# One layer of a flow-matching backbone on one core: x transposed by token tile between the adaLN slabs, constant products on TensorE, and the second adaLN slabs in other buffers

## The chip, the core and the metric

The kernel runs on one core of one Trainium2 chip. The metric is the device time of one execution, in microseconds (us). Before the change it was measured three times: 1683.73, 1684.34 and 1685.08, median 1684.34. The profile shows one more execution of 1684.17 us; its span, from the first to the last instruction, is 1682.5 us. Engines are named as in the profile: PE (TensorE), DVE (VectorE), ACT (ScalarE), POOL (GpSimd) and SP, whose queue issues most DMAs.

## The reference

One layer is applied to 128 context tokens and 256 latent tokens of width 2048. Only the start matters here: the adaLN modulation, the first norm and the input projection.

```python
def _adaln(cond, ada_w, ada_b):
    mod = jax.nn.silu(cond) @ ada_w + ada_b
    return mod.reshape(cond.shape[0], N_MOD, D_MODEL)
...
    shift_a, scale_a, gate_a, shift_f, scale_f, gate_f = [mod[:, i][:, None, :] for i in range(N_MOD)]
    h = _rmsnorm(x, norm_w[0]) * (1 + scale_a) + shift_a
    proj = h @ w_in
    q, k, v, o, g, u = jnp.split(proj, [M, 2 * M, 3 * M, 4 * M, 4 * M + N_GATES * N_HEADS], axis=-1)
...
    mix = jnp.concatenate([hm, hp], axis=-1) @ w_out
    x = x + gate_a * _rmsnorm(mix, norm_w[1])
    h = _rmsnorm(x, norm_w[2]) * (1 + scale_f) + shift_f
    y = jnp.square(jax.nn.relu(h @ w1)) @ w2
    x = x + gate_f * _rmsnorm(y, norm_w[3])
```

The condition is `c_ctx` for the context tokens and `c` for the latent ones; `ada_w` is 2048 x 12288. All inputs are float32.

## The kernel before

All 384 tokens are worked on together: three token tiles of 128, and 16 feature tiles of 128. Every large product is made of three products of split numbers (high x high, high x low, low x high); a weight tile or h is split by ACT, which writes the high half, and DVE, which subtracts to get the low half (L135 and L136 for weights, L448 and L449 for h).

The opening. SP issues the loads of the two conditions (L80, L81), of the constants (L82: identity, ones and a selector) and of x (L88, 1 MB for each token tile). POOL issues the loads of the parameters. Then come the adaLN slabs, 512 KB each: four slabs hold the 16 x 128 rows of one pair of feature tiles of `ada_w` for one of scale and shift. Function `ada_mat` multiplies a slab with cT, the conditions after silu, in four small products that lie side by side on PE (L257; the profile counts two rows for each float32 product, so x8 is one slab). Function `ada_rows` then copies the sums out of PSUM on ACT (L269), and two small products (L273) add the four groups and turn them; `ada_finish` adds the bias on DVE (L281, L286). The result is `mod`. The generator `first_ada` strings these pieces together and stops after each slab; `next(ada0)` runs it to its next stop. The string `X_ORDER` says when: "a" is one such piece, "t" transposes one feature tile of x for the three token tiles (three PE transposes, L403, into one PSUM bank, and a copy of 384 columns by DVE or ACT, L411 and L409), and "b" spreads the inverse norms `rx` over a row, a diagonal matrix on DVE (L207, `dg_rx`) and a product with ones on PE (L209, `bc_rx`), copied to `rbc` (L424).

Function `make_h(s)` makes h for the two feature tiles of step s: `hm` = xT x mod x rbc on DVE (L443), then high and low halves `hh` and `hl`. Steps s = 0 to 7 run over pairs of feature tiles, and in each step five chunks of output columns (u 512, u 512, v 384, v 384, v 256 with the 32 gate columns) are multiplied for three token tiles (L503: 18 products a chunk). In the first step the sums are copied out by ACT (L522), later ones are added by DVE (L524). Weight tiles are loaded ahead by `load_ahead` into three raw buffers, so a load waits until the split of the third one before it is done.

Within the first step the rest of x is transposed after the first chunk (twelve transposes), then the first four slabs for step 1 are multiplied, and four more after the first v chunk. `ADA_STEPS` gives the pieces per chunk. The slabs of step 1 share four buffers (`adap`, named ada_raw). From step 2 on, `ada_eight` takes eight slabs for scale and shift, four of them in the free half of the u tiles and in the tile of the masks (`spare`), four in `adap`.

The order on PE, DVE and ACT is written out by hand up to the end of `make_h(0)`; from there on only PE's is, and the order on DVE and ACT is made by a scheduler. Each engine runs its instructions in order, SP its issues too. At most eight DMAs of SP are under way, since its ninth waits for the semaphore of the first.

## Time and profile before

| quantity | value |
|---|---|
| median of three runs | 1684.34 us |
| profiled execution, its span | 1684.17 us, 1682.5 us |
| ACT busy | 751.3 us, 45% of the span |
| POOL busy | 133.3 us, 8% of the span |
| first product of the projection (u, L503) starts | 29.84 us |
| second step of the projection starts (u, L503) | 53.05 us |
| PE busy, 0 to 15 us | 1.71 us |
| PE busy, 30 to 120 us | 90.00 us |
| DMA share, 10 to 35 us | 0.99 to 1.10 |

A row of the timeline gives the start and the busy time of a group of equal instructions, the engine and line, what is written and read, and how many; in brackets stands the idle time of the engine ahead of it and what ended it. Matmul rows overlap, so the cost of one on PE is the distance from its start to the next start. A row of the chain gives start, length and what the time was spent on. A row of the waits gives who waited for whom, the sum, the number and the longest. Rows of DMA issues end with the time from issue to landing.

### The profile page before, as it was taken

What the parts mean: (1) busy time and instruction counts of PE and PEld (TensorE: products, weight loads), DVE (VectorE), ACT (ScalarE), POOL (GpSimd) and SP (SyncE); (2) the same over time, 40 slices, a digit from 0 to 9 for tenths busy, and PEclk for the clock granted to TensorE, in tenths of its full rate; (3) what the DMA queues carried; (4) which work ended last, traced back from release to release, by engine and by line L of the source; (5) the groups of instructions that cost most, each with busy time, mean ns of one, the idle gap of its engine ahead of it and who ended that gap; (6) DMA issues with size and microseconds to landing.
All of it is one profiled execution on the core that took longest, in us unless ns stands there. A gap on an engine that the chain in (4) does not pass through costs nothing.

```text
span 1682.5 us, 27870 instructions
## 1 busy us (share of the span) xinstructions
PE 1654.3 (98%) x10965; PEld 1581.4 (94%) x10965; DVE 1340.3 (80%) x2009; ACT 751.3 (45%) x1225; POOL 133.3 (8%) x185
## 2 busy tenths in 40 slices
PE   6999999999999999999999999999999999999997
PEld 3888999999999989989999999999999999999996
DVE  3677769898999959997897688988588588588688
ACT  5322355555443345543444444444444444445443
POOL 1000002221000024520000000000000000000120
PEclk9999999999999999999999999999999999999999
DMA  9999757786789954754546246444344443443653
GB/s 318 332 310 298 253 172 248 240 258 221 238 273 311 311 194 142 209 151 128 178 154 195 84 135 187 152 144 150 101 151 129 123 138 118 145 124 113 186 182 136
DMA packets 258099, 320.95 MB, mean 191 GB/s; under 512 B 14784, under 2 KB 223120, under 8 KB 257584
## 3 DMA queue, kind: packets, MB, share of 16 engines
q1 hardware_dynamic: 250688, 303.62, 57.1%
q0 software_dynamic: 5984, 13.78, 2.9%
q8 instruction: 86, 1.41, 0.4%
q10 hardware_dynamic: 1296, 1.77, 0.3%
q14 instruction: 45, 0.37, 0.1%
HBM read 308.61 MB, written 10.51 MB: 190 GB/s over the span
## 4 chain that ended last, share of the span: by engine, by line
PE 94%; DVE 3%; issue 1%; DMA 1%; ACT 0%; SPq 0%; POOL 0%; DVEq 0%; ACTq 0%; POOLq 0%
PE acc_w L145 10%; PE acc_w L144 10%; PE acc_w L146 10%; PE v L503 4%; PE y L1231 4%; PE y L1232 4%; PE y L1230 4%; PE u L503 4%; PE acc_wo L144 3%; PE acc_wo L145 3%; PE acc_wo L146 2%; PE y_yz L1231 2%; PE y_yz L1230 2%; PE y_yz L1232 2%; PE y L1074 2%; PE y L1073 2%
## 5 line engine op out<-in xcount | busy, mean ns | idle before, releaser
L145 PE MATMUL acc_w<-h2l,hi_w 128*128 128x384 f32 (+1 forms) x1024 | 346.2, 338 | 0.5 <-DVE h2l L1024 0.5
L144 PE MATMUL acc_w<-h2h,hi_w 128*128 128x384 f32 (+1 forms) x1024 | 344.2, 338 | 1.2 <-ACT h2h L1020 1.2
L146 PE MATMUL acc_w<-h2h,lo_w 128*128 128x384 f32 (+1 forms) x1024 | 345.1, 337 | 0.0
L136 DVE TENSOR_TENSOR lo_w<-raw_w,hi_w 128x1024 fp32r<-128x1024 f32 x152 | 185.3, 1220 | 136.5 <-ACT hi_w L135 136.3
L135 ACT ACTIVATE hi_w<-raw_w 128x1024 fp32r<-128x1024 f32 x152 | 160.8, 1058 | 213.7 <-PE acc_w L145 83.4
L317 DVE SCALAR_TENSOR_TENSOR ada_acc<-ada_raw,sg,ada_acc 128x1024 f32<-128x1024 f32 (+1 forms) x240 | 252.0, 1081 | 2.1 <-DMA ada_raw<-in_ada_w_dram 2.1
L144 PEld LDWEIGHTS acc_w<-h2h,hi_w 128*128 128x128 f32 x1024 | 192.2, 188 | 2.9 <-ACT h2h L1020 2.0
L145 PEld LDWEIGHTS acc_w<-h2l,hi_w 128*128 128x128 f32 x1024 | 192.6, 188 | 1.2 <-DVE h2l L1024 0.8
L146 PEld LDWEIGHTS acc_w<-h2h,lo_w 128*128 128x128 f32 x1024 | 192.4, 188 | 0.3 <-DVE lo_w L136 0.2
L1216 ACT ACTIVATE hi_t<-w 128x1024 fp32r<-128x1024 f32 x104 | 109.5, 1059 | 118.7 <-PE y L1232 34.0
L1217 DVE TENSOR_TENSOR lo_t<-w,hi_t 128x1024 fp32r<-128x1024 f32 x104 | 126.3, 1220 | 15.1 <-ACT hi_t L1216 14.7
L1217 DVE TENSOR_TENSOR lo_b<-w,hi_b 128x1024 fp32r<-128x1024 f32 x78 | 95.3, 1221 | 40.0 <-ACT hi_b L1216 39.8
L1216 ACT ACTIVATE hi_b<-w 128x1024 fp32r<-128x1024 f32 x78 | 82.5, 1060 | 97.0 <-PE acc_w L145 64.6
L135 ACT ACTIVATE hi_wo<-raw_wo 128x1024 fp32r<-128x1024 f32 x32 | 34.0, 1064 | 81.3 <-DMA raw_wo<-in_w_out_dram 64.0
L950 ACT ACTIVATE z<-acc_w 128x384 f32<-128x384 f32 x54 | 26.3, 487 | 74.8 <-PE acc_w L146 74.8
L503 PE MATMUL v<-hi_v,hh 128*128 128x384 f32 (+1 forms) x144 | 47.8, 332 | 0.0
L503 PE MATMUL v<-lo_v,hh 128*128 128x384 f32 (+1 forms) x144 | 46.5, 323 | 0.0
L503 PE MATMUL v<-hi_v,hl 128*128 128x384 f32 (+1 forms) x144 | 46.5, 323 | 0.0
L136 DVE TENSOR_TENSOR lo_wo<-raw_wo,hi_wo 128x1024 fp32r<-128x1024 f32 x32 | 38.8, 1218 | 7.3 <-ACT hi_wo L135 6.3
L986 POOL DMA_DIRECT2D gf_dram<-gfT x1 | 0.5, 521 | 551.9 <-DVE gfT L985 551.9
L144 PE MATMUL acc_k<-hh,hi_k 128*128 128x384 f32 x128 | 44.2, 345 | 0.0
L144 PE MATMUL acc_o<-hh,hi_o 128*128 128x384 f32 x128 | 43.9, 343 | 0.0
(2268 smaller groups left out, 4566.9 us busy)
## 6 DMA issues: line engine op xcount, KB each, us to landing
raw_w<-in_w_dram SPq DMA_DIRECT2D x152, 512.0 KB, 4.3
ada_raw<-in_ada_w_dram SPq DMA_DIRECT2D x130, 512.0 KB, 5.0
w<-in_w_dram SPq DMA_DIRECT2D x104, 512.0 KB, 4.4
raw_wo<-in_w_out_dram SPq DMA_DIRECT2D x32, 512.0 KB, 5.6
u<-in_ada_w_dram SPq DMA_DIRECT2D x18, 512.0 KB, 6.0
raw_u<-in_w_in_dram SPq DMA_DIRECT2D x16, 512.0 KB, 7.0
raw_q<-in_w_in_dram SPq DMA_DIRECT2D x16, 512.0 KB, 4.7
raw_k<-in_w_in_dram SPq DMA_DIRECT2D x16, 512.0 KB, 4.7
```

Source lines behind the costliest of these rows:

```text
L135: nc.scalar.activation(hi[:, 0:n], raw[:, 0:n], AF.Copy)
L136: low = lambda: nc.vector.tensor_tensor(lo[:, 0:n], raw[:, 0:n], hi[:, 0:n].bitcast(F32), op=ALU.subtract)
L144: nc.tensor.matmul(ps, lh, rh, start=start, stop=False)
L145: nc.tensor.matmul(ps, lh, rl, start=False, stop=False)
L146: mm3.ins = nc.tensor.matmul(ps, ll, rh, start=False, stop=stop).ins
L317: nc.vector.scalar_tensor_tensor(acc[:, g, :], raw[:, a, :], cj, acc[:, g, :], op0=ALU.mult, op1=ALU.add)
L503: nc.tensor.matmul(acc[i][:, 0:n], h[k0 + k][a][:, i * P:(i + 1) * P], (hi, lo)[b][:, k, :], start=k == 0 and a + b == 0, stop=k == nk - 1 ...
L1216: nc.scalar.activation(hi, raw, AF.Copy)
L1217: nc.vector.tensor_tensor(lo, raw, hi.bitcast(F32), op=ALU.subtract)
L1230: nc.tensor.matmul(acc, xh, wh, start=start and j == 0, stop=False)
L1231: nc.tensor.matmul(acc, xh, wl, start=False, stop=False)
L1232: nc.tensor.matmul(acc, xl, wh, start=False, stop=stop and j == 3)
```

## The change

x of the first token tile is now the first load of SP; the constants come through ACT's queue. x is transposed by token tile: one call of `transpose_x` turns four feature tiles of one token tile into one bank, with four copies of 128 columns. Products of constants without use for their result (`run_up`: of the zeroed `rbc` at the start, of the constants tile later; letter "z" in `X_ORDER`) are put between slabs and transposes. All transposes of x are made ahead of the first chunk. `hm` of step 0 is made as soon as scale is there (letter "h"). The first weight tile is loaded and split in two halves. The second four slabs of step 1 go to the free places (`spare`) and no longer wait for the `adap` buffers, and `ada_eight` uses `adap` first and `spare` second. In step 0 the slab groups of step 1 are multiplied after the second and the fourth chunk, and `make_h(1)` is made within the fifth chunk. `AHEAD` gives the number of weight tiles loaded ahead in step 0.

```diff
-ADA_STEPS = (4, 0, 4, 0, 0)
-X_ORDER = "tatatatattaatabata"
+ADA_STEPS = (0, 4, 0, 4, 0)
+AHEAD = (1, 1, 3, 2, 3)
+X_ORDER = "azaxabzaxzahaxzaxzaxzaxz"
...
-    nc.sync.dma_start(cc[:, 0, :], c_ctx.rearrange("(p j) -> p j", j=16))
-    nc.sync.dma_start(cc[:, 1, :], c[0].rearrange("(p j) -> p j", j=16))
-    nc.sync.dma_start(cst[:, 0:3], cs_src[:, 0:3])
+    nc.scalar.dma_start(cst[:, 0:3], cs_src[:, 0:3])
...
+    nc.sync.dma_start(x_tok[0], x_prompt[0])
+    nc.sync.dma_start(cc[:, 0, :], c_ctx.rearrange("(p j) -> p j", j=16))
+    nc.sync.dma_start(cc[:, 1, :], c[0].rearrange("(p j) -> p j", j=16))
+    for i in (1, 2):
+        nc.sync.dma_start(x_tok[i], x_sample[0, (i - 1) * P:i * P])
...
-                yield from ada_mat([(0, k0, nk), (1, k0, nk)])
+                some = [adap.tile([P, 4, 256], F32, tag="ada", name=f"ada_raw_0_{k0}_{j}", bufs=N_ADA) for j in range(0, 16, 4)]
+                yield from ada_mat([(0, k0, nk), (1, k0, nk)], into=(some, spare))
...
-                raw = (spare.pop(0) if len(raws) < 4 else
+                raw = (spare.pop(0) if len(raws) >= 4 else
...
+    def run_up(n, src=None, w=NTOK):
+        src = cst.rearrange("p n q -> p (n q)") if src is None else src
+        for _ in range(n):
+            nc.tensor.matmul(run[:, 0:w], src[:, 0:P], src[:, 0:w], start=True, stop=True)
...
+    def transpose_x(i, k0, on_act, later=False):
+        ps = bank(f"xt_{i}_{k0}")
+        for a in range(4):
+            nc.tensor.transpose(ps[:, a * P:(a + 1) * P], x_tok[i][:, (k0 + a) * P:(k0 + a + 1) * P], ident)
+
+        def copy():
+            for a in range(4):
+                dst, src = xT[k0 + a][:, i * P:(i + 1) * P], ps[:, a * P:(a + 1) * P]
...
+    run_up(6, rbc)
+    squares(0)
+    for q in range(2):
+        transpose_x(0, 4 * q, False)
+    run_up(1)
...
+    squares(1)
+    transpose_x(1, 0, False)
+    squares(2)
+    run_up(3)
+    transpose_x(2, 0, False)
...
+    next(ada0)
+    for _ in range(2):
+        transpose_x(*x_rest.pop(0))
+    run_up(1)
+    h_ins = make_h(0, scaled)
+    nc.vector.tensor_tensor(lo0, raw0, hi0.bitcast(F32), op=ALU.subtract)
...
+                        if s == i == k == 0 and ci == 4:
+                            with tc.high_priority():
+                                next(ada0)
+                                make_h(1)
...
-            if s == 0 and ci == XT_AT:
-                while len(xT) < KT:
-                    transpose_x(len(xT))
...
-            if ci == 3 and s < NS - 1:
+            if ci == 3 and 0 < s < NS - 1:
                 make_h(s + 1)
```

Three places show how rows move. The first is PE, from the seventh slab (the third for shift) to the first product of u; xtok_89 to _91 are the token tiles before, xtok_87 to _89 after. Before:

```order
L257 MATMUL ada_0_206<-ada_raw_0_8_230,cT 32x256 x4
L403 MATMUL xt_236<-cst,xtok_89 128x128
L403 MATMUL xt_236<-cst,xtok_90 128x128
L403 MATMUL xt_236<-cst,xtok_91 128x128
L257 MATMUL ada_0_206<-ada_raw_0_12_242,cT 32x256 x4
L403 MATMUL xt_271<-cst,xtok_89 128x128
L403 MATMUL xt_271<-cst,xtok_90 128x128
L403 MATMUL xt_271<-cst,xtok_91 128x128
L403 MATMUL xt_276<-cst,xtok_89 128x128
L403 MATMUL xt_276<-cst,xtok_90 128x128
L403 MATMUL xt_276<-cst,xtok_91 128x128
L273 MATMUL ada_0_206<-cst,ada_sb_0_248 128x2 x2
```

Six more transposes and u follow there. The same place in the changed kernel:

```order
L261 MATMUL ada_0_270<-ada_raw_0_8_303,cT 32x256 x4
L406 MATMUL xt_8_309<-cst,xtok_89 128x128 x4
L395 MATMUL run<-cst 128x256
L261 MATMUL ada_0_270<-ada_raw_0_12_319,cT 32x256 x4
L406 MATMUL xt_12_327<-cst,xtok_89 128x128 x4
L395 MATMUL run<-cst 128x256
L277 MATMUL ada_0_270<-cst,ada_sb_0_325 128x2 x2
L406 MATMUL xt_8_351<-cst,xtok_87 128x128 x4
L406 MATMUL xt_12_356<-cst,xtok_87 128x128 x4
L395 MATMUL run<-cst 128x384
L533 MATMUL u_0_0_384<-hi_u_first,hh_261 128x512
```

Four transposes and a product of constants follow each slab, and eight transposes and a wider product of constants stand between the last small product and u.

The second place is PE at the end of step 0: the last slab of step 1, then products of v, and the small product that adds the sums. Before (the other nine products of this chunk, of 384 columns, and the 18 of the last chunk, of 288, follow):

```order
L257 MATMUL ada_2_361<-ada_raw_2_12_471,cT 32x256 x4
L503 MATMUL v_0_0_488<-hi_v_0_397,hh_262 128x384
L503 MATMUL v_0_0_488<-hi_v_0_397,hl_263 128x384
L503 MATMUL v_0_0_488<-lo_v_0_398,hh_262 128x384
L503 MATMUL v_0_1_489<-hi_v_0_397,hh_262 128x384
L503 MATMUL v_0_1_489<-hi_v_0_397,hl_263 128x384
L503 MATMUL v_0_1_489<-lo_v_0_398,hh_262 128x384
L503 MATMUL v_0_2_490<-hi_v_0_397,hh_262 128x384
L503 MATMUL v_0_2_490<-hi_v_0_397,hl_263 128x384
L503 MATMUL v_0_2_490<-lo_v_0_398,hh_262 128x384
L273 MATMUL ada_2_361<-cst,ada_sb_2_477 128x4 x2
```

After:

```order
L261 MATMUL ada_2_439<-u_339,cT 32x256 x4
L261 MATMUL ada_2_439<-masks,cT 32x256 x4
L533 MATMUL v_0_0_564<-hi_v_0_478,hh_261 128x288
L533 MATMUL v_0_0_564<-hi_v_0_478,hl_262 128x288
L533 MATMUL v_0_0_564<-lo_v_0_479,hh_261 128x288
L277 MATMUL ada_2_439<-cst,ada_sb_2_547 128x4 x2
L533 MATMUL v_0_1_565<-hi_v_0_478,hh_261 128x288
```

Before, 27 products of v (9 of 384 columns, 18 of 288) stood between the small product and u of step 1; now 15 of 288 columns do.

The third place is DVE right after that small product, where `mod`, the split of u's second weight tile for step 1, `hm` and `hl` follow each other. Before:

```order
L281 TENSOR_TENSOR mod<-ada_2_361,prmT 128x4 x2
L286 SCALAR_TENSOR_TENSOR mod<-mod,prmT 128x4
L136 TENSOR_TENSOR lo_u_1_485<-raw_u_1_482,hi_u_1_484 128x1024
L443 SCALAR_TENSOR_TENSOR hm_514<-xT_168,mod,rbc 128x128
L443 SCALAR_TENSOR_TENSOR hm_514<-xT_168,mod,rbc 128x256
L443 SCALAR_TENSOR_TENSOR hm_519<-xT_180,mod,rbc 128x128
L443 SCALAR_TENSOR_TENSOR hm_519<-xT_180,mod,rbc 128x256
L449 SCALAR_TENSOR_TENSOR hl_516<-hm_514,mod,hh_515 128x128
```

After:

```order
L285 TENSOR_TENSOR mod<-ada_2_439,prmT 128x4 x2
L290 SCALAR_TENSOR_TENSOR mod<-mod,prmT 128x4
L139 TENSOR_TENSOR lo_u_1_561<-raw_u_1_558,hi_u_1_560 128x1024
L445 SCALAR_TENSOR_TENSOR hm_575<-xT_128,mod,rbc 128x128
L445 SCALAR_TENSOR_TENSOR hm_575<-xT_128,mod,rbc 128x256
L445 SCALAR_TENSOR_TENSOR hm_580<-xT_129,mod,rbc 128x128
L445 SCALAR_TENSOR_TENSOR hm_580<-xT_129,mod,rbc 128x256
L478 SCALAR_TENSOR_TENSOR hl_577<-hm_575,mod,hh_576 128x128
```

The sequence is the same, with one difference: the weight split that stands in it is of u's second tile instead of its first.

## The prediction

> **What bounds the kernel now.** I read the page's busy shares first, then TensorE's (PE's) waits over the whole run, the chain that ended last, and the PE timeline up to the first product of the input projection.

> ```profile
> PE 1654.3 (98%) x10965; PEld 1581.4 (94%) x10965; DVE 1340.3 (80%) x2009; ACT 751.3 (45%) x1225; POOL 133.3 (8%) x185
> ...
> PE xt L403 <- DMA xtok<-in_x_sample_dram: 4.8, 2, 2.8
> PE pp L379 <- DMA cst<-in_consts_dram: 4.5, 1, 4.5
> PE pp L380 <- DMA prm<-in_pool_scale_dram: 4.0, 1, 4.0
> ...
> PE ada L257 <- DMA ada_raw<-in_ada_w_dram: 1.1, 1, 1.1
> ...
> PE bc_rx L209 <- DVE dg_rx L207: 0.5, 1, 0.5
> ```

> PE is busy 1654.3 of 1682.5 us, and of its 28.2 idle us these rows hold 14.9, all before 25.4 us. So nearly everything behind the opening moves with the moment at which the first product of the projection, u at L503, starts, and with PE's work and waits after it. I call that moment T0; it is 29.84 us.

> ```profile
> 12.29 0.47 PE L403 MATMUL xt<-cst,xtok 128*128 128x128 f32 x1 [2.85 <-DMA xtok<-in_x_sample_dram]
> 14.73 0.47 PE L403 MATMUL xt<-cst,xtok 128*128 128x128 f32 x1 [1.98 <-DMA xtok<-in_x_sample_dram]
> 16.32 1.08 PE L257 MATMUL ada<-ada_raw,cT 128*32 128x256 f32 x8 [1.11 <-DMA ada_raw<-in_ada_w_dram]
> 17.34 0.90 PE L403 MATMUL xt<-cst,xtok 128*128 128x128 f32 x3
> 18.17 1.08 PE L257 MATMUL ada<-ada_raw,cT 128*32 128x256 f32 x8
> ...
> 22.71 0.51 PE L273 MATMUL ada<-cst,ada_sb 128*128 128x2 f32 x4
> 23.15 0.64 PE L257 MATMUL ada<-ada_raw,cT 128*32 128x256 f32 x8
> 23.72 0.55 PE L403 MATMUL xt<-cst,xtok 128*128 128x128 f32 x3
> 24.20 0.64 PE L257 MATMUL ada<-ada_raw,cT 128*32 128x256 f32 x8
> 25.38 0.91 PE L209 MATMUL bc_rx<-dg_rx,cst 128*128 128x384 f32 x2 [0.55 <-DVE dg_rx L207]
> 26.22 0.64 PE L257 MATMUL ada<-ada_raw,cT 128*32 128x256 f32 x8
> ...
> 29.84 1.37 PE L503 MATMUL u<-hi_u,hh 128*128 128x512 f32 x4
> ...
> 34.29 1.47 PE L403 MATMUL xt<-cst,xtok 128*128 128x128 f32 x12
> 35.69 1.93 PE L257 MATMUL ada<-ada_raw,cT 128*32 128x256 f32 x32
> 37.55 0.50 PE L503 MATMUL u<-hi_u,hh 128*128 128x512 f32 x1
> ...
> 41.84 0.34 PE L503 MATMUL v<-hi_v,hh 128*128 128x384 f32 x1
> ```

> From one start to the next these rows give prices: a slab of adaLN weights 0.57 us (23.15 to 23.72), three transposes 0.48, twelve 1.40, so one more transpose 0.10, four 0.58 and eight 0.99; the full-array product of 384 columns 0.84; the small product L273 0.44. The first slabs took 1.02 us (16.32 to 17.34) and three transposes 0.83: PE ran at about half its rate until 20.5 us, though the clock column of the page shows full clock there.

> **When the slabs come.** The second slab was issued at 4.25 and took 13.5 us to land, so about 17.7; the first landed at 3.61 + 12.58 = 16.19, and they follow each other by 1.5 us, so the eighth landed near 26.7.

> ```profile
> 3.61 12.58 DMA ada_raw<-in_ada_w_dram
> ...
> 4.25 0.65 SPq L253 DMA_DIRECT2D ada_raw<-in_ada_w_dram  x1
> ada_raw<-in_ada_w_dram SPq DMA_DIRECT2D x1, 512.0 KB, 13.5
> ...
> 0.81 0.38 SPq L80 DMA_DIRECT2D cc<-in_c_ctx_dram  x1
> 2.18 0.43 SPq L88 DMA_DIRECT2D xtok<-in_x_prompt_dram  x1
> ```

> The change issues x first, at 0.81 instead of 2.18: 1.37 us earlier at most. The 192 KB of constants (0.55 us at 512 KB in 1.5 us) and the two small loads of c now share the stream, so I take 0.6 us, between 0 and 1.37. Slab 2 then lands at 17.1, slab 3 at 18.6, slab 8 at 26.1.

> **The opening, added up.** The change puts a product of constants (256 columns) at seven places between slabs, one of 384 columns before u, and all 48 transposes before u. The trace has no product of 256 columns on the full array; the nearest rows are 2/3 of the 384-column one, 0.56, and a slab's two passes of 256 columns less the switch, 0.46. I take 0.46 behind transposes, 0.54 beside slabs, and 0.72 for 384 columns (0.69 to 0.84). A round of slab, four transposes and constants is then 0.57 + 0.58 + 0.46 = 1.61 us, more than the 1.5 us in which a slab comes. **The rests that the constants are to fill are not there from slab 4 on.**

> Before that, VectorE (DVE) holds the rms product back. Its order puts four copies of 128 columns ahead of dg_rx.

> ```profile
> 9.26 0.26 DVE L381 COPY prmT<-pp 128x96 f32<-128x96 f32 x1 [3.45 <-PE pp L380]
> 9.44 0.23 DVE L382 COPY prmT<-pp 128x80 f32<-128x80 f32 x1
> ...
> 24.78 0.55 DVE L207 TENSOR_TENSOR dg_rx<-cst,rx 128x384 f32<-128x384 f32 x1
> ```

> Four such copies cost about 0.86 (0.19 apart, 0.29 the last; never less than 0.8 by these rows, never more than 2.2 by the 0.56 of 384 columns). Slab 2 runs at 17.15, its transposes from 17.72 to 18.4, the copies to 19.25, dg_rx to 19.8, bc_rx starts at 19.85. PE was ready at 19.2 and waits 0.6. Then: bc_rx 0.84 and constants 0.54 to 21.23; slab 4, transposes, constants and small product 2.05 to 23.28; slabs 5 to 7, 3 x 1.61, to 28.11; slab 8 with the same four 2.05 to 30.16; eight transposes 0.99 to 31.15; constants 0.72 to **T0 = 31.87, 2.03 later**. The first weight tile and its halves are ready well before that, so loading it in two DMAs gains nothing; the scaling of h moved ahead lies beside PE's work.

> From T0 on PE loses the twelve transposes, 1.40 us. The first 18 products took 4.45 us (29.84 to 34.29), the next 18 4.29 (37.55 to 41.84): with h split in good time 0.16 goes. The second slabs of step 0 land in free places about 1 us earlier than now; nobody waits for them now, so this is 0.

> **The end of step 0** is where the change adds a wait. The second slabs' group moves behind two more v chunks, and the small product stands 15 products ahead of the next step instead of 27.

> ```profile
> 48.65 0.50 PE L273 MATMUL ada<-cst,ada_sb 128*128 128x4 f32 x4
> 50.68 0.29 PE L503 MATMUL v<-hi_v,hh 128*128 128x288 f32 x1
> 53.05 0.39 PE L503 MATMUL u<-hi_u,hh 128*128 128x512 f32 x1
> ...
> 49.61 1.23 DVE L136 TENSOR_TENSOR lo_u<-raw_u,hi_u 128x1024 fp32r<-128x1024 f32 x1
> 50.75 1.40 DVE L443 SCALAR_TENSOR_TENSOR hm<-xT,mod,rbc 128x128 f32<-128x128 f32 x4
> 52.07 1.04 DVE L449 SCALAR_TENSOR_TENSOR hl<-hm,mod,hh 128x128 fp32r<-128x128 f32 x3
> ```

> Now DVE needs from 48.65 to 52.07 + 0.35 = 52.42, 3.77 us, for mod, a weight split (lo_u), four scalings (hm) and the first low half (hl). That row sequence is unchanged: the weight split still stands ahead of hm, its high half now behind the copy of the adaLN sums on ScalarE (ACT). PE then reaches the second u product, which needs hl, 0.37 + 15 x 0.13 + 0.23 = 2.57 us after the small product starts (18 of 288 columns took 2.37). **It waits 3.77 + 0.05 - 2.57 = 1.25 us**, between 0.8, if DVE finishes the split sooner, and 1.6. ACT's copies of the last v accumulators stand ahead of hh and cost the first product 0.9 of the same wait. Behind PE everything of step 1 is queued. The small product itself waits 0.1 for its copy, with only three products in front of it.

> **Sum:** +2.03 - 1.40 - 0.16 + 0.10 + 1.25 = +1.8 us. The profiled execution took 1684.17 (span 1682.5 and 1.67 around it), 0.17 below the median of 1684.34, so 1685.97; I say **1686.0**. Differences within 0.2%, 3.4 us, are about what a measurement of this kernel cannot tell from no change.

> **Rivals.** *The rests hold.* If a constant product costs far less than its columns say, PE keeps up with the slabs. Even so slab 8's group, eight transposes and constants follow its landing: 26.18 + 2.05 + 0.99 + 0.72 = 29.94, and the sum is -0.1 (1684.1); with the full advance of 1.37 it is 1683.3, and without the wait at u 1682.1. Against it: the 384-column row, 0.84. 17 in 100.

> *The clock falls back; slower.* PE is warmed by six products of 384 columns from about 1.4 us, the first three at half rate (3 x 1.45 + 3 x 0.72, to 7.9); eight transposes, constants and the two transposes of the parameters end near 10. It rests 1.7 us for x of the second token tile (12.29 less 0.6), and about 0.6 before slab 1. If these rests return it to half rate, slab 1 costs 1.02, constants 0.97, slab 2 1.02 and four transposes 1.04: the copies start at 19.8 instead of 18.4, and T0 is 1.4 to 1.5 later: 1687.5, and 1688.9 if slab 4's group too is slow. It decides when the first slab's row reads 1.08 instead of 0.64. Before has no rest after the rate rose but 0.55 us, so no row excludes it. 16 in 100.

> [...] Transposes ran at the higher rate here (0.48 against 0.83), but no row shows whether they keep it.

> *The queue of DMA issues (SP) blocks step 1:* five slabs and two v loads of step 1 now stand behind a v load whose buffer is free only when DVE has split u's weights, near 51 (now 49.61 + 1.23). They take some 10 us of the stream behind what is under way, so they land by 63; the group that uses them comes 11.5 us after u of step 1 (36 products of 0.23, 18 of 0.18), near 66. The 3 us of slack speak against it; if they are gone the time is 1688 or more; 4 in 100. *Faster than all this,* 3 in 100: eight transposes and constants at the end would have to be free.

> **How the numbers follow.** My forecast, 1685.0 to 1687.2, has 60 in 100. The range 1682.6 to 1688.1 leaves out the bottom of the first rival and the top of the second, some 13 in 100. Slower by over 0.2% (above 1687.7) is the upper half of the clock rival, the blocked queue and a little of the forecast: 0.12. Faster by over 0.2% (below 1681.0): 0.03. Within: 0.85.

> **What would show it.** Right: u starts near 31.9; PE has no idle between slab 4 and u; bc_rx waits about 0.6 for dg_rx; the first two u products of step 1 wait 1.25 together for hh and hl; no transposes after u; the rest of the timeline shifted by a constant. Wrong: PE waits for slabs 5 to 8 (constants cheap), the first slab's row reads 1.08 (clock), or no wait before step 1.

## The result, and the profile after the change

The changed kernel took 1690.41 us, median of 6 runs (1689.02 to 1692.2). The kernel before took 1684.93 in 6 runs made beside them (1683.73 to 1686.29). The ratio is 1.0033 with a 95% interval of 1.002 to 1.0046: slower by some 5.5 us, where the prediction said 1.66 slower (1686.0 less 1684.34), and outside its range of 1682.6 to 1688.1. A second measurement of the unchanged text gave 1689.8 against 1685.4, ratio 1.003 [1.0018, 1.0042], so the loss measured is 4.4 to 5.5 us. The profiled execution took 1689.02, its span is 1687.3.

The first line of the page and PE's waits in the first 70 us (the sum, the number, the longest) answer to the rows before:

```profile
PE 1666.9 (99%) x11001; PEld 1589.0 (94%) x11001; DVE 1344.2 (80%) x2038; ACT 749.8 (44%) x1230; POOL 133.2 (8%) x185
...
PE xt L406 <- DMA xtok<-in_x_sample_dram: 1.8, 1, 1.8
PE run L395 <- DVE rbc L108: 1.4, 1, 1.4
PE u L533 <- ACT hh L477: 1.3, 1, 1.3
PE bc_rx L212 <- DVE dg_rx L210: 0.8, 1, 0.8
PE pp L427 <- DMA prm<-in_pool_scale_dram: 0.2, 1, 0.2
```

The waits for slabs are gone, and PE's idle time has fallen from 28.2 to 20.4 us (1687.3 less 1666.9). PE is not done earlier for it: it is busy 12.6 us longer, of which the six products ahead of everything take 5.52 (the first row below). Less idle time on the bounding engine is no gain where work without use fills it.

The PE timeline of the opening and of the start of step 1, with the columns of the rows before:

```profile
1.45 5.52 PE L395 MATMUL run<-rbc 128*128 128x384 f32 x12 [1.45 <-DVE rbc L108]
...
15.64 0.64 PE L261 MATMUL ada<-ada_raw,cT 128*32 128x256 f32 x8
...
19.50 0.91 PE L212 MATMUL bc_rx<-dg_rx,cst 128*128 128x384 f32 x2 [0.80 <-DVE dg_rx L210]
20.25 0.59 PE L395 MATMUL run<-cst 128*128 128x256 f32 x2
20.78 0.64 PE L261 MATMUL ada<-ada_raw,cT 128*32 128x256 f32 x8
...
22.70 0.64 PE L261 MATMUL ada<-ada_raw,cT 128*32 128x256 f32 x8
23.27 0.66 PE L406 MATMUL xt<-cst,xtok 128*128 128x128 f32 x4
23.77 0.60 PE L395 MATMUL run<-cst 128*128 128x256 f32 x2
24.29 0.64 PE L261 MATMUL ada<-ada_raw,cT 128*32 128x256 f32 x8
...
28.97 0.50 PE L277 MATMUL ada<-cst,ada_sb 128*128 128x2 f32 x4
29.33 1.07 PE L406 MATMUL xt<-cst,xtok 128*128 128x128 f32 x8
30.24 0.81 PE L395 MATMUL run<-cst 128*128 128x384 f32 x2
30.59 1.98 PE L533 MATMUL u<-hi_u_first,hh 128*128 128x512 f32 x6
39.50 1.93 PE L261 MATMUL ada<-ada_raw,cT 128*32 128x256 f32 x32
...
54.26 0.50 PE L533 MATMUL u<-hi_u,hh 128*128 128x512 f32 x1 [1.25 <-ACT hh L477]
54.65 0.50 PE L533 MATMUL u<-hi_u,hl 128*128 128x512 f32 x1
54.99 0.40 PE L533 MATMUL u<-lo_u,hh 128*128 128x512 f32 x1
...
69.71 0.45 PE L533 MATMUL v<-hi_v,hh 128*128 128x384 f32 x1
```

From 20.78 to u no row has a bracket: PE no longer waits for slabs but works at its own pace, a round of slab, transposes and constants taking 1.59 us (22.70 to 24.29). u starts at 30.59, not 29.84; before step 1 stands the new wait of 1.25. The v product at 69.71 started at 68.20 before: the opening and step 0 together cost 1.51 us in this pair of profiles.

```profile
68.20 0.45 PE L503 MATMUL v<-hi_v,hh 128*128 128x384 f32 x1
```

The spans differ by 4.8 us, so some 3 us of the loss arose later, in code that the change hardly touches.

### The profile page after: what moved, and what is told of

Same layout as the page of the kernel before. It is cut to its first block, busy times and chain, and to the rows that moved or that the text cites. A ratio compares the mean times of both kernels' runs of the same rounds, so it can differ in the third digit from the quotient of the medians.

```text
span 1687.3 us, 27974 instructions
## 1 busy us (share of the span) xinstructions
PE 1666.9 (99%) x11001; PEld 1589.0 (94%) x11001; DVE 1344.2 (80%) x2038; ACT 749.8 (44%) x1230; POOL 133.2 (8%) x185
## 4 chain that ended last, share of the span: by engine, by line
PE 86%; DVE 7%; DMA 4%; issue 2%; ACT 1%; POOL 0%; SPq 0%; DVEq 0%; ACTq 0%; POOLq 0%
PE acc_w L147 9%; PE acc_w L148 9%; PE acc_w L149 9%; PE v L533 4%; PE u L533 4%; PE y L1262 4%; PE y L1263 4%; PE y L1261 4%; PE acc_wo L147 2%; PE acc_wo L149 2%; PE acc_wo L148 2%; PE y_yz L1261 2%; PE y_yz L1262 2%; PE y_yz L1263 2%; PE y L1105 2%
## 6 DMA issues: line engine op xcount, KB each, us to landing
raw_w<-in_w_dram SPq DMA_DIRECT2D x152, 512.0 KB, 4.1
ada_raw<-in_ada_w_dram SPq DMA_DIRECT2D x126, 512.0 KB, 4.8
w<-in_w_dram SPq DMA_DIRECT2D x104, 512.0 KB, 4.3
raw_wo<-in_w_out_dram SPq DMA_DIRECT2D x32, 512.0 KB, 5.7
u<-in_ada_w_dram SPq DMA_DIRECT2D x21, 512.0 KB, 8.3
raw_q<-in_w_in_dram SPq DMA_DIRECT2D x16, 512.0 KB, 4.4
raw_k<-in_w_in_dram SPq DMA_DIRECT2D x16, 512.0 KB, 4.9
raw_o<-in_w_in_dram SPq DMA_DIRECT2D x16, 512.0 KB, 4.7
```

## The experiments

Seventeen runs followed, two of them of the unedited kernels. "At 66", "at 520", "at 800" and "at 1600" give how many us later the same PE product starts in one profile than in the first profile of the kernel before, near these times. These four columns are worked out from the starts of single products, one execution each, and the start of step 0 alone differs from one profile to another by up to 2.2 us in kernels with the same opening (b_eight, b_slots); the medians are of 5 to 12 timed runs.

```
label         median   ratio [95%]               at 66  at 520  at 800  at 1600
after         1690.41  1.0033 [1.0020, 1.0046]    1.51    2.03    4.05    4.88
a_again       1689.80  1.0030 [1.0018, 1.0042]    2.04    2.13    3.97    5.65
a_noz         1686.76  1.0012 [1.0003, 1.0022]    0.29     .94    1.17    1.28
a_step0       1688.55  1.0018 [1.0009, 1.0027]    0.34    1.28    2.78    4.88
a_step0_noz   1686.33  1.0005 [0.9997, 1.0014]    0.09    1.65    3.17    3.97
a_hearly      1690.99  1.0037 [1.0024, 1.0049]    1.93    2.74    4.40    5.05
a_eight       1692.39  1.0045 [1.0033, 1.0058]    1.35    1.83    5.22    8.80
a_apart       1692.57  1.0041 [1.0028, 1.0054]    2.24    2.34    7.63    7.18
a_lay1        1689.26  1.0026 [1.0016, 1.0036]    1.73    2.38    5.01    4.51
a_lay3        1691.15  1.0032 [1.0021, 1.0043]    1.91    2.45    5.24    8.98
b_again       1686.18  1.0004 [0.9995, 1.0012]    1.12    2.23    3.60    4.79
b_shift2      1687.80  1.0015 [1.0007, 1.0024]    1.00    1.47    3.14    3.82
b_shift5      1688.29  1.0019 [1.0010, 1.0027]    2.74    3.49    4.95    4.11
b_eight       1685.31  1.0001 [0.9992, 1.0010]    -.76     .21    1.89    0.62
b_apart       1686.44  1.0008 [1.0000, 1.0017]     .77     .76    1.17    1.33
b_slots       1685.52  1.0002 [0.9993, 1.0010]    1.46    1.63    1.53    2.86
b_lay3        1686.43  1.0005 [0.9997, 1.0014]    -.36    -.51    -.50    -.07
b_xfirst      1684.28  0.9991 [0.9982, 1.0000]    -.53     .08     .22    -.21
```

Labels with a_ start from the changed kernel, with b_ from the one before. The kernel before took 1685.05, 1685.4, 1685.52, 1685.38 and 1685.56 in the five groups of runs. The median of a_lay3 is that of seven runs; an eighth took 9366.91 us and is left out.

### Does a later start alone cost more than itself?

Two or five products of constants ahead of step 1 of the kernel before.

```diff
+            if s == 1 and ci == 0:
+                for _ in range(2):
+                    nc.tensor.matmul(acc[0][:, 0:NTOK], cst[:, 0, :], cst.rearrange("p n q -> p (n q)"), start=True, stop=True)
```

> The kernel before, with two products of constants (384 columns, 0.84 us each by the trace of before) put ahead of the first product of step 1: TensorE stands about 1.7 us later from 53 us on, as far as the changed kernel stands (+1.5 us at 66), and nothing else is touched. Theory 1 (the transfers and splits of the output projection react to where TensorE stands): 1.7 plus the 1.5 to 3.5 us that the changed kernel lost behind the projection, so 1688 to 1690.5, with TensorE waiting for lo_wo near 525 us. Theory 2 (the extra comes from the other places of the second slabs, or from the order of the issue queue): 1.7 alone, 1686.6, and no wait at lo_wo. Theory 3 (that wait is chance): 1.7 alone in most runs, and single runs 2 us longer.

> The same with five products, 4.2 us. Theory 1: the wait at lo_wo depends on the size of the shift, so the sum is not 4.2: either more than 1690.5 or, if weights get ahead again, less than 1688.5. Theories 2 and 3: 1689.1, two and a half times what the kernel with two products gains over the kernel before.

The two cost 1.32 us where they stand, the five 3.26: 0.65 each, not the 0.84 that was expected. The times rose by 2.75 and 3.24, and neither profile has a wait for `lo_wo` near 525 us. The first lost more than was put in, the second did not; on average a shift of everything behind step 0 adds 0.7 to itself, with about 1 of uncertainty. So a pure shift does not explain the 3 us of the changed kernel.

### The constants, and the order of step 0

The seven products of constants of 256 columns between the slabs, taken out; those at the start, around x and the one ahead of u stay:

```diff
-X_ORDER = "azaxabzaxzahaxzaxzaxzaxz"
+X_ORDER = "aaxabaxahaxaxaxax"
```

> The changed kernel without the seven products of constants of 256 columns between the slabs. My theory (TensorE is overloaded from slab 4 on, rounds of 1.59 against 1.5 us): the rounds fall under the stream, TensorE waits again for slabs 5 to 8, and after slab 8 at 25.5 come 0.6 + 0.6 + 0.4 + 1.0 + 0.35: the first u product at about 28.5 instead of 30.6, 2 us earlier, and the time about 2 us less than the changed kernel, 1688.4, if the later part moves along. Rival (the products of constants hold the rate up): the first slabs take 1.0 instead of 0.6 us each, u is at 30.6 or later, no gain.

The PE timeline of this kernel at the same place:

```profile
26.36 0.64 PE L261 MATMUL ada<-ada_raw,cT 128*32 128x256 f32 x8 [0.28 <-DMA ada_raw<-in_ada_w_dram]
...
28.03 1.07 PE L406 MATMUL xt<-cst,xtok 128*128 128x128 f32 x8
28.94 0.81 PE L395 MATMUL run<-cst 128*128 128x384 f32 x2
29.29 1.89 PE L533 MATMUL u<-hi_u_first,hh 128*128 128x512 f32 x5
```

PE waits for slabs again, u follows the landing of slab 8 (26.32) by 2.97 instead of 5.05 (slab 8 of the profile after landed at 25.54), and the rate is not lost: the slab's row reads 0.64, as with constants. u itself starts only 1.30 earlier than in the profile after, since the slabs came later in this execution. Over all profiles u starts at 31.00 on average with the constants (eight profiles) and at 29.29 and 29.21 without: the constants cost some 1.7 us at u, close to the 1.93 between the prediction's T0 and the one of its first rival. The time fell by 3.0 to 3.65 us against the two measurements of the changed kernel, more than the 2 that were expected.

Then the order of step 0 of the kernel before in the changed kernel: both slab groups back in their places, and `make_h(1)` behind the fourth chunk.

```diff
-ADA_STEPS = (0, 4, 0, 4, 0)
+ADA_STEPS = (4, 0, 4, 0, 0)
...
-                        if s == i == k == 0 and ci == 4:
-                            with tc.high_priority():
-                                next(ada0)
-                                make_h(1)
-                    if s > 0 and ci == 3 and k == 0:
+                    if ci == 3 and k == 0:
...
-            if ci == 3 and 0 < s < NS - 1:
+            if ci == 3 and s < NS - 1:
```

> The changed kernel with the order of step 0 as before: the first slabs' group behind the first u chunk, the second behind the first v chunk, the small product in the middle of the second v chunk and h of step 1 made behind it. The waits at u of step 1 (1.25 for hh, 0.43 of stalls behind it) should be gone; the second group may wait some 0.8 us for its last slab (it lands at 46.9, the group would come at 44.6 and reach that slab 1.4 later). So 0.9 to 1.7 us less by 66 us than the changed kernel, and the time 1688.3 to 1689.1 if what is behind moves along; if the later part takes it back, 1690.

At 66 us this kernel stands at 0.34 where the changed one stands at 1.51, though its u started later (31.34 against 30.59): from u to 66 us the changed order costs 1.9 us, and the wait before step 1 is the largest part of it. The time was 1688.55, 1.3 to 1.9 us less than the two measurements of the changed kernel.

Both edits together:

> The changed kernel without the seven products of constants and with step 0 in the order of before. Each alone gave 1686.8 and 1688.6. By the opening: u at about 29.0 (as without the constants), no wait at u of step 1, but the second group of slabs is reached 2 us earlier than with the constants while its last slab lands near 47 all the same, so it waits 2 to 3 us there and most of one gain is lost: 1686 to 1687. If the two add, 1685.2 or less, as fast as the kernel before.

1686.33, within what was expected and 0.95 above the kernel before, in an interval that holds no change. So the constants and the order of step 0 carry most of the loss. In both pairs, without constants against with them, the time fell by more than the opening explains: a_noz 3.0 to 3.65 with 1.2 to 1.75 at 66 us, a_step0_noz 2.2 with 0.25. So some 2 us seem to go with the constants in a way that the place of u does not show. Through what was not found; each of these medians is known to some 1.5 us only, and the columns are single executions.

A third way to the wait: the second slab group in the middle of the first v chunk, so that the small product and `make_h(1)` come ahead of the last chunk.

```diff
-ADA_STEPS = (0, 4, 0, 4, 0)
+ADA_STEPS = (0, 4, 0, 0, 0)
...
-                        if s == i == k == 0 and ci == 4:
-                            with tc.high_priority():
-                                next(ada0)
-                                make_h(1)
-                    if s > 0 and ci == 3 and k == 0:
-                        next(ada0, None)
+                    if ci == 3 and k == 0:
+                        for _ in range(1 if s else 4):
+                            next(ada0, None)
...
+            if s == 0 and ci == 3:
+                with tc.high_priority():
+                    next(ada0)
+                    make_h(1)
```

> The changed kernel, with the second slabs' group of step 0 in the middle of the v chunk before, and the small product and the scaling and splitting of h for step 1 ahead of the last v chunk: TensorE has 18 products instead of 15 before u of step 1, and DVE's splits of weights stand the same way. My theory: the wait at u of step 1 (1.25 us for hh, and 0.27 us of stalls at the next two products) falls to 0 to 0.4, the time to about 1689.2, 1.2 us less, if the later part moves along. Rival (what TensorE gains there the later waits take back): no change against 1690.4.

A miss: 1690.99, no gain. The timeline of PE, and under it of DVE, at the start of step 1:

```profile
53.80 0.50 PE L533 MATMUL u<-hi_u,hh 128*128 128x512 f32 x1 [0.36 <-ACT hh L477]
...
55.78 0.50 PE L533 MATMUL u<-hi_u,hl 128*128 128x512 f32 x1 [0.57 <-DVE hl L478]
...
53.85 0.34 DVE L478 SCALAR_TENSOR_TENSOR hl<-hm,mod,hh 128x128 fp32r<-128x128 f32 x1
54.12 1.22 DVE L139 TENSOR_TENSOR lo_u<-raw_u,hi_u 128x1024 fp32r<-128x1024 f32 x1
55.25 1.14 DVE L478 SCALAR_TENSOR_TENSOR hl<-hm,mod,hh 128x256 fp32r<-128x256 f32 x3
```

The weight split of 1.22 us now stands between the first `hl` and the next. The wait of 1.25 became 0.36 and 0.57, and at 66 us this kernel stands no better than the changed one (1.93).

### What differs from one execution to the next

The changed kernel again, unedited, and the kernel before again, unedited:

> The changed kernel once more, with nothing edited, for a second profile and more runs. In its first profile TensorE lost 1.5 us to 66 us, another 1.8 at the wait for lo_wo at 524 us, and 1.6 in smaller pieces. Theory 'chance': the wait at lo_wo is gone or elsewhere, or the granted clock falls for 3.4 us near 544 us as it did in three of the four experiments so far, while the median stays near 1690. Theory 'fixed': the same wait at the same place, 1.5 us again. The drift of about 1 us in steps under 0.01 us between 390 and 1430 us belongs to the kernel if it comes again.

> The kernel before once more, for a second profile. Theory 'the later waits are the changed kernel's own': it stays within 1.5 us of its first profile between 66 and 1600 us, with at most one fall of the clock (1.55 us) among it. Theory 'they come by chance to both': it shows 2 us or more.

The second profile of the kernel before has a span of 1687.3, the first one 1682.5, and the profile after 1687.3 too. The execution of this second profile is the slowest of eleven (1688.97 us). So the kernel before can show on its own all of the 4.8 us in which the profiles of before and after differ. In the opening it loses 1.12, with the first slab landing at 17.09 instead of 16.19. Its waits on PE name two more places:

```profile
PE y L1231 <- DVE lo_t L1217: 1.5, 1, 1.5
...
PE mb L678 <- ACT hnT L791: 0.8, 1, 0.8
```

The fourth place shows only in PE's clock. The windows of this second profile (columns: window, its length, busy time and count of PE, weight load, DVE, ACT and POOL, granted PE clock, DMA share, GB/s):

```profile
542.00:544.00 2.00, 1.60 (x12) 1.60 (x13) 2.00 (x3) 1.11 (x3) 0.00 (x0) 1.00 1.07 373
544.00:546.00 2.00, 2.00 (x10) 2.00 (x9) 2.00 (x8) 0.39 (x1) 0.00 (x0) 0.63 1.05 381
546.00:548.00 2.00, 2.00 (x8) 2.00 (x7) 2.00 (x4) 1.04 (x5) 0.00 (x0) 0.52 1.10 349
548.00:550.00 2.00, 2.00 (x14) 2.00 (x13) 2.00 (x3) 0.00 (x0) 0.00 (x0) 1.00 1.11 359
```

PE is busy throughout from 544, but makes 8 products in 2 us instead of 14, at a clock of 0.52. The clock fell to half for 3.41 us and cost about 1.55. Just ahead stand two groups of very small products and one wait:

```profile
540.71 0.95 PE L273 MATMUL ada_gate<-cst,ada_sb 128*128 128x4 f32 x8
542.40 1.06 PE L336 MATMUL adaf<-cst,adav_sb 128*128 128x4 f32 x8 [0.75 <-ACT adav_sb L332]
```

Both kernels have this light stretch of 2.75 us (in the first profile of before it starts at 538.48). The clock fell there in 10 of the 17 profiles with this stretch unedited, those of a_apart and b_apart left out: not in the first profiles of before and after, but in a_again and b_again. The timed runs agree: of 120 runs of the kernel before, the 27 with a mean clock of 0.997 average 1686.44, the 83 with 0.998 average 1685.17, the ten with 0.999 average 1684.73.

To break up this stretch, a large product was put between the two small groups.

```diff
...
+        if i == 3 and c == 1024:
+            with tc.issue_after(ada_rows.ins):
+                for _ in range(1):
+                    nc.tensor.matmul(pf[:, 0:NTOK], ident, cst.rearrange("p n q -> p (n q)"), start=True, stop=True)
```

> The changed kernel with the two small groups of products at 542 us (the gate's L277 and adaf) set apart: one product of constants of 384 columns, 0.65 us, is added, and by it the list scheduler puts the small groups some 70 products later, with products of weights between them, so that no wait of 0.75 us and no light stretch of 2.9 us is left there. If the clock falls at this stretch in the usual execution of the changed kernel (1.55 us each time), the time falls by 1 to 1.6 us to about 1689; if it falls there seldom, by 0.1 (0.75 less 0.65).

> The same edit in the kernel before. If the clock falls at this stretch as often as in the changed kernel, it gains as much (1683.5 to 1684); if before is spared because of where it stands then, it gains 0.1 (1685). Theory 'the stretch makes part of the difference': it gains at least 0.8 us less than the changed kernel does by the same edit.

A miss. The scheduler put the groups elsewhere, and in a_apart `adaf` waits 2.2 us where it waited 0.75; in b_apart that wait stays at 0.7:

```profile
PE adaf L344 <- ACT adav_sb L336: 2.2, 1, 2.2
```

In a_apart the clock then fell for 6.83 us at once; in the profile of b_apart it did not fall there, and the median was still not better (1686.44 against 1685.4). That no wide product can help is not shown by it.

### The slabs of steps 2 to 7

The order in which `ada_eight` uses its buffers, put into the kernel before, and taken out of the changed one:

```diff
-                raw = (spare.pop(0) if len(raws) < 4 else
+                raw = (spare.pop(0) if len(raws) >= 4 else
...
-                if len(raws) < 4:
+                if len(raws) >= 4:
```

> The kernel before with one part of the change alone: in steps 2 to 7 the first four slabs of a group go to the adaLN tiles and the second four to the free places, not the other way round. DVE and ACT keep their orders to the row; SyncE's order changes a little, and the first 128x1024 slab of the next stage is issued three loads earlier. The changed kernel loses some 2 us behind the projection that neither the opening nor the addresses explain. Theory 'issue order': this kernel loses them too, 1687 and above. Theory 'not the issue order': no difference to before, 1685 within 0.8.

> The changed kernel with that part taken back (free places first in steps 2 to 7). Theory 'issue order': 2 us less than the changed kernel, 1688. Theory 'not the issue order': 1690 again; a wait for the second slabs in step 1 of some tenths is possible, as the free places are in use until 50 us there.

Into the kernel before: no effect (1.0001 [0.9992, 1.001]). Out of the changed kernel: worse, not better, 1692.39, with a wait of PE of 2.4 that ends at 904.4 us:

```profile
PE y_yz L1262 <- DVE lo_b L1248: 2.4, 1, 2.4
```

The first profile after has 0.7 in that row. Right behind this wait the clock of a_eight fell once more, at 904.31 for 3.41 us. So the buffer order is not what was lost behind step 0.

### Where the tiles lie

From 390 to 1430 us the changed kernels without further buffers fall back by 0.6 to 0.8 us in steps below 0.02 us for each product, with no wait and no fallen clock in it. One or three unused buffers were added, with a write of eight numbers each, which moves the addresses of the tiles behind them (one buffer is shown; in b_slots VectorE writes it):

```diff
+    sp0 = slot("spare_slot0")
+    nc.gpsimd.memset(sp0[0:1, 0:8], 0.0)
```

> The kernel before with one tile more taken from the pool of slots at the start (and given back after a write of eight numbers), so that some 15 percent of TensorE's operands lie at other addresses of SBUF later, as they do in the changed kernel, and nothing else changes. If the slow drift of the changed kernel (about 1 us between 390 and 1430 us, in steps under 0.01 us a product, which the kernels made from before don't show) comes from the addresses, this kernel drifts against before by some tenths of a us too, in either direction. If it doesn't drift, the drift comes from something else.

> The same with one tile more: a third layout of the changed kernel. Same numbers as for the kernel with three.

> The changed kernel with three more tiles taken from the pool of slots at the start (three writes of eight numbers on GpSimd), so that the tiles behind lie at other addresses, and nothing else. Theory 'addresses': the later part's share (3 to 3.5 us of the 4.9) moves with them: the median differs from 1690 by 1 us or more, and the slow drift between 970 and 1430 us has another course. Theory 'not the addresses': 1690 within 0.7, whatever the drift does.

> The kernel before with three tiles more. Theory 'addresses': its own layout is a lucky one, and this one is slower by 0.5 us or more, with a drift against before of some tenths to 1 us. Theory 'not the addresses': 1685.3 within 0.5.

Kernels with the addresses of before (b_again, b_shift2, b_shift5, b_eight, b_xfirst) do not drift against it: b_again stands at 4.79 both at 950 and at 1600. Those with other addresses drift each in its own way: b_slots from 2.00 at 950 to 2.86, b_lay3 from -1.11 to -.07, a_lay1 from 4.55 to 4.51. The starts of the single products show it best. Between 950 and 1430 us the five kernels with the addresses of before repeat its spacing from product to product within 2 ns. All kernels with the layout of after, whatever their opening, depart from it by the same sum, 0.63 us; b_lay3 departs by 0.75, b_slots by 0.80, a_lay3 by 0.66 and a_lay1 by 0.21. So the addresses are worth some tenths of a us up to 0.8. The medians of the four lie 0.1 to 1.4 us from those of the kernels that they start from, and a_lay1 is still 3.9 above before: the layout does not explain the rest.

### The part that may help

Into the kernel before, only the first idea of the change: x first on SP, the constants on ACT's queue.

```diff
-    nc.sync.dma_start(cc[:, 0, :], c_ctx.rearrange("(p j) -> p j", j=16))
-    nc.sync.dma_start(cc[:, 1, :], c[0].rearrange("(p j) -> p j", j=16))
-    nc.sync.dma_start(cst[:, 0:3], cs_src[:, 0:3])
+    nc.scalar.dma_start(cst[:, 0:3], cs_src[:, 0:3])
...
-    for t, src in zip(x_tok, (x_prompt[0], x_sample[0, 0:128], x_sample[0, 128:256])):
-        nc.sync.dma_start(t, src)
+    nc.sync.dma_start(x_tok[0], x_prompt[0])
+    nc.sync.dma_start(cc[:, 0, :], c_ctx.rearrange("(p j) -> p j", j=16))
+    nc.sync.dma_start(cc[:, 1, :], c[0].rearrange("(p j) -> p j", j=16))
...
```

> The kernel before with one part of the change alone: the first tile of x loaded first on SyncE and the constants on ScalarE's queue. In the profiles so far the changed kernels' first slab landed at 15.0 to 15.8 us, those of the kernels with the old order at 15.8 to 17.6, 0.75 apart in the mean. If the opening waits for the stream of slabs in the old layout (TensorE waits 1.1 us for the first slab there), u starts some 0.75 us earlier and the time is 1684.6 against 1685.4; if the transposes' layout (three tiles of x for each) holds it, no gain.

1684.28 against 1685.56, ratio 0.9991 [0.9982, 1.0]. This is the lowest median of all kernels here, 1.3 us below before with an interval that just touches no change. Its PE timeline:

```profile
15.70 1.08 PE L258 MATMUL ada<-ada_raw,cT 128*32 128x256 f32 x8 [1.12 <-DMA ada_raw<-in_ada_w_dram]
...
29.31 1.83 PE L504 MATMUL u<-hi_u,hh 128*128 128x512 f32 x6
```

Slab 1 runs 0.62 us earlier than in the first profile of before, u 0.53. One profile can't decide it: among the eight profiles with the old order u starts between 29.08 and 31.28, and this one has 29.31.

## Why the prediction was wrong

**The opening and step 0: right in sum, by luck.** u was to start at 31.87, 2.03 later than before; it started at 30.59, 0.75 later (0.9 in the means of all profiles with either opening, 30.91 against 30.01). From u to 66 us the sum had -0.21; the profiles show +0.76. Two errors of about 1 us cancel: 1.8 was predicted at this point, the first pair shows 1.51 and the means 1.6.

In the opening the mechanism was right: a round was to take 1.61 and took 1.59, the wait at `bc_rx` was to be 0.6 and is 0.8, and there is no idle time between slab 4 and u. Part of the 1.28 by which u came sooner is that the slabs landed 1.2 us earlier than before, not 0.6 (the first at 14.99, not 16.19; over all profiles it is 0.8). Another 0.45 lies in the small product and the constants at the end: 0.36 us (28.97 to 29.33) for a step taken at 0.44, 0.35 (30.24 to 30.59) for one taken at 0.72.

In step 0 the twelve transposes went, as said. But the gain of 0.16 in the first 36 products did not come: from u to 39.50 they took 8.91, where 4.45 + 4.29 = 8.74 stood before. The wait at u of step 1 was to be 1.25 for hh and hl together; the row for hh alone has that, and 0.16 + 0.11 of stall follow at the next two, since a product of 512 columns takes 0.23 (53.05 to 53.28 before; the steps from 54.26 to 54.65 and 54.99 are 0.39 and 0.34). Most of the rest lies around the small product, where three v products take 0.57 (49.74 to 50.31) instead of three steps of 0.13.

**The step that failed: "the rest of the timeline shifted by a constant"**, the term behind step 0 that the sum put at nothing. Behind 66 us the changed kernels lost another 4.1 us on average in nine profiles (1.0 to 7.5), against 1.4 in eight profiles of the kernels made from before (0 to 3.7, the first profile of before itself with 0), both counted from the first profile of before and without a_apart and b_apart. The difference, 2.7 us, divides by place (worked out from the starts of single products; means of all nine and all eight):

```
place in us   what is lost                           changed   old
390 to 1430   drift with the addresses                 0.5     0.1
524           wait for lo_wo (3 of 9; 0 of 8)          0.4     0
542           fall of the clock (6 of 9; 4 of 8)       1.2     0.8
676           over 1 us for r2bc (2 of 9; 0 of 8)      0.3     0
800 to 950    waits for lo_t and lo_b                  1.0    -0.1
```

The fall of the clock comes to both kinds; that it came more often to one may be chance. The last row holds the second fall in a_eight.

The wait at 524 in the profile after, PE and then DVE:

```profile
526.01 0.33 PE L148 MATMUL acc_wo<-mx12l,hi_wo 128*128 128x384 f32 x1
527.88 0.44 PE L149 MATMUL acc_wo<-mx12h,lo_wo 128*128 128x384 f32 x1 [1.54 <-DVE lo_wo L139]
...
526.14 0.56 DVE L912 TENSOR_TENSOR sqa<-sqa,sq_mo 128x384 f32<-128x384 f32 x1 [2.80 <-ACT sq_mo L911]
526.61 1.22 DVE L139 TENSOR_TENSOR lo_wo<-raw_wo,hi_wo 128x1024 fp32r<-128x1024 f32 x1
```

DVE stands idle 2.80 us for ACT's squares, while the weight split that PE needs is queued behind them. Before, the same split ran from 521.88 and PE had no wait (523.98, 524.15). The squares in turn stand on ACT behind `hi_wo`, which waits for a load of 512 KB; first the rows after, from the chain and from ACT's timeline, then ACT's row before:

```profile
517.45 7.11 DMA raw_wo<-in_w_out_dram
524.67 1.06 ACT L138 ACTIVATE hi_wo<-raw_wo 128x1024 fp32r<-128x1024 f32 x1 [4.42 <-DMA raw_wo<-in_w_out_dram]
...
519.94 1.06 ACT L135 ACTIVATE hi_wo<-raw_wo 128x1024 fp32r<-128x1024 f32 x1 [3.78 <-DMA raw_wo<-in_w_out_dram]
```

This load took 7.11 us after, 6.74 in a_lay3 and 5.77 in a_lay1, the three profiles that lose time here, and 4.4 to 5.5 in all others (5.06 before). The wait for `lo_b` near 901 us has such a load behind it too; the rows of the chain, after and in a_lay3:

```profile
892.67 4.76 DMA w<-in_w_dram
...
895.36 6.18 DMA w<-in_w_dram
```

PE's wait for `lo_b` is 0.71 and 2.11 there, and in all 19 profiles it is this load's time less 4.0 to 4.1 us. The load took 5.1 us on average in the ten profiles of changed kernels and 4.6 in the nine of the kernels made from before. So at both places PE waits because one weight load lands late. In a_again the wait at 524 is gone and the clock falls instead, so the loss of one execution is not that of the next.

What is settled: opening and step 0 cost about 1.6 us at 66 us, by the constants and by the order of step 0. Taking out the constants starts u 1.7 us sooner, the old order saves 1.9 from u on; the two do not add (0.29 and 0.34 at 66 us alone, 0.09 together), and without both the kernel is within the noise of the one before. The addresses cost 0.6 to 0.8. **What stays open** is some 2 us: why the loads behind the waits at 524 and near 901 take longer in the changed kernels, and why taking the constants out saves some 2 us more than at u. It is not the buffer order of `ada_eight` alone, and a pure shift gives only 0.7 of it. The spread within a kind is larger than the difference, so the shares by place are rough; the difference itself stands on the timed medians.

**The base.** The sum was made from one execution and three runs, 1684.34. Over 126 runs the kernel before has a median of 1685.3 and reaches from 1682.78 to 1688.54. That puts about 1 us of the miss into the base, and a range of 5.5 us around a single profile was narrow for a program whose own executions differ by 5.8. The prediction also took 3.4 us as what a measurement cannot tell from no change; the intervals here are 1.5 to 2.2 us to each side.

**The rivals.** The first slab's row reads 0.64, so the clock rival is not what happened. That the clock can fall on a short rest, which it rested on, was right (below): it fell in the opening in six of the ten profiles of changed kernels, in the one after from 11.10 to 14.51, behind a wait of 1.77 us for x, but was back when the first slab, which had landed at 14.99, ran at 15.64. The sum had put the rests of 1.7 us at no cost, and no run shows that: the three products of constants behind this wait took 3.26 us (11.85 to 15.11), most of it at a clock of 0.50. The blocked queue did not come: no wait for a slab stands at 66 us. That the rests hold is out as well, since a_noz shows what the constants cost.

## What to carry to other kernels

Filling an engine's rests pays only as long as the rests exist: compare the round, with the filler, to the interval at which the data come (here 1.59 us against 1.5), and take the fillers out where the round is the longer one. A move that brings a producer closer to its consumer has to be counted on the producer's queue, with what else stands there: here a weight split of 1.22 us stood between h and the product that needed it, wherever h was put. For a forecast of some tenths of a per cent, two or three profiles of the kernel before come first, since what differs between them is no smaller than the change.

## What the runs showed of the hardware that was not expected

```profile
12.00:13.00 1.00, 1.00 (x3) 0.53 (x2) 0.99 (x6) 0.97 (x3) 0.00 (x0) 0.50 0.94 362
13.00:14.00 1.00, 1.00 (x3) 0.57 (x2) 0.00 (x0) 0.97 (x3) 0.00 (x0) 0.50 1.09 385
...
15.00:16.00 1.00, 1.00 (x13) 0.52 (x11) 0.25 (x2) 0.97 (x2) 0.00 (x0) 1.00 1.10 349
```

**Where only the addresses differed, PE's pace moved by 0.75 us (b_lay3) and 0.80 (b_slots) in 480, and with one layout it repeats to 2 ns.** Between 950 and 1430 us the step from one product to the next is the same within 2 ns in six kernels with one layout (before, b_again, b_shift2, b_shift5, b_eight, b_xfirst). Where the tiles lay elsewhere, nine in ten steps of the same products in the same order were 6 ns shorter to 7 ns longer, and single ones up to 18 shorter or 28 longer; over these 480 us that sums up to 0.2 to 0.8 us.
